# A fifth Strassen chunk per SwiGLU, with the products reordered and the next norms moved between them

## Chip, cores and metric

The kernel runs on one core of a Trainium2 chip. The metric is the device time of one execution in microseconds (us); before the change its median over 3 runs is 1292.14 us (1290.93 to 1292.8).

## The reference, cut to what matters

One decoder layer on 512 tokens of width 1024, all in float32. Two SwiGLU sub-layers stand around a token mixer:

```python
def swiglu(x, w_gate, w_up, w_down):
    return (jax.nn.silu(x @ w_gate) * (x @ w_up)) @ w_down

x = x + 0.5 * swiglu(rms_norm(x, ffn1_norm), ffn1_w_gate, ffn1_w_up, ffn1_w_down)
x = x + token_mixer(rms_norm(x, mix_norm), w_in, ...)
x = x + 0.5 * swiglu(rms_norm(x, ffn2_norm), ffn2_w_gate, ffn2_w_up, ffn2_w_down)
```

The hidden width of a SwiGLU (D_FF) is 2816, that is 22 blocks of 128.

## The kernel before

**Arithmetic.** Every float32 product of matrices is made of three matmuls (`mm3`, line 502): each operand is split into a high part (rounded to fp32r) and a low part (the rest), and high x high, high x low and low x high are added up in PSUM. So each weight tile is first split: ScalarE (ACT) writes the high part `whi` (line 106), and VectorE (DVE) or GpSimd (POOL) subtracts it from the raw tile to get the low part `wlo` (line 107). The order on each engine is that in which the Python code issues its instructions; nothing is moved by a scheduler.

**The SwiGLU (`ffn`, line 564).** Pass p = 0 to 10 of the loop at line 659 makes 256 hidden columns: two "gate" blocks g0, g1 and two "up" blocks u0, u1, of 24 matmuls each (128 x 128 by 128 x 512). `act_g` and `act_u` turn each pair into a hidden block `a` (line 583), which is split in turn into the left operands of the down projection. The 22 hidden blocks are multiplied with w_down in two ways:

- Blocks 0 to 15 in four **chunks** of four blocks each, by Strassen's seven products over a 2 x 2 cut of (tokens: tiles 0, 1 / tiles 2, 3) and (output columns: 0 to 511 / 512 to 1023). A product (`down_block`, line 633) is 2 groups of 6 matmuls and is added to one or two quarters of x (`INTO`, line 631; `add_x`, line 643). Chunk c is worked off in passes 2c + 2 and 2c + 3, one product behind each gate or up block (4 in the even pass, 3 in the odd). Its weights come through `Blocks` (line 127): two raw tiles of 1 MB each, seven parts, of which some are sums or differences of quarters that POOL computes ahead of the split (`sum`, line 149; `after`, line 152); the low parts of these weights are always made on POOL (line 93).
- Blocks 16 to 21 plainly (`down_tile`, line 646): blocks 16 and 17 (weights d4) within pass 10, 48 matmuls between g1 and u0; blocks 18 to 21 (weights d5_0, d5_1) in the closing loop at line 699, 24 matmuls for each of the four token tiles.

**The order of the splits.** `plan` lists all weight parts in the order in which PE uses them. `W.get` (line 115) issues every split up to the part asked for, if that has not been done; `W.bg(n)` (line 121) issues one more split, if no more than n parts beyond the current one have been issued. Within a SwiGLU each block and each product calls it once with n = 2, so that splits are issued two parts ahead of their use; in pass 10 it is called with n = 4, twice for each up block. `whi` and `wlo` have four buffers each; the parts in `W.held` (line 397) go to buffers of the large pool in their place. So a split can wait for the matmuls of the part that had its buffer, and what is queued behind it on ACT or DVE waits with it. In `down_block` the call of `W.bg` (line 636) stands ahead of the product's matmuls and additions.

**Between the first SwiGLU and the mixer.** When a token tile of x is whole, `after1` (line 742) queues three stages in `nstage`: `norm_1` (sum of squares on ACT, mean on DVE, a power on POOL), `norm_2` (two multiplications on DVE that write h) and `norm_3` (eight transposes `nt` on PE, split into hmh and hml by ACT and DVE). Each `tick` runs the next stage of every queued tile. The closing loop calls `tick` twice for each token tile, and `W.bg(4)` behind it. The mixer begins with `proj_c` (line 797), whose weights are the parts of c0 and c1. Behind the second SwiGLU `after2` only writes the tile out. PSUM has three banks for each of `mm` (line 265) and `sc` (line 268); `down_tile` and one half of `down_block` use `sc`, and a bank is free again when its additions on DVE are done.

Of the kernel before, what the change touches and what calls it, by code (L numbers as in the profile page):

```python
# [12 lines left out]
F32R = mybir.dt.float32r  # L13
AF = mybir.ActivationFunctionType
ALU = mybir.AluOpType
# [5 lines left out]
NT = SEQ // 128  # L21
# [105 lines left out]
class Blocks:  # L127
# [15 lines left out]
    def part(self, p):  # L143
        if p == 0:
            self.spare = self.new_spare()
            self.sum(self.spare, self.b12, self.b22, ALU.subtract)
        return (self.spare, self.b11, self.b22, self.spare, self.b12, self.b11, self.b21)[p]

    def sum(self, out, a, b, op):
        self.nc.gpsimd.tensor_tensor(out, a, b, op=op)  # L150
# [1 line left out]
    def after(self, p):  # L152
        if p == 1:
            self.sum(self.spare, self.b11, self.b22, ALU.add)
        elif p == 2:
            self.sum(self.b12, self.b11, self.b12, ALU.add)
        elif p == 3:
            self.sum(self.b11, self.b21, self.b11, ALU.subtract)
        elif p == 4:
            self.sum(self.b21, self.b21, self.b22, ALU.add)  # L160
        elif p == 6:
            self.then()

# [70 lines left out]
def drain(g):  # L234
    for _ in g:
        pass
# [8 lines left out]
def hybrid_trunk_kernel(ctx: ExitStack, tc: tile.TileContext, x, rel_bias, ffn1_norm, ffn1_w_gate, ffn1_w_up,  # L245
# [28 lines left out]
    def t4(name, dt=F32):  # L274
        return big.tile([128, 1024], dt, tag="t4", name=name)
# [12 lines left out]
    specs, plan, blocks = [], [], {}  # L288
# [20 lines left out]
    def rows(w, name, r0, nk, c0, nc_):  # L309

        src = w[r0:r0 + nk * 128, c0:c0 + nc_].rearrange("(k p) c -> p k c", p=128)
        loads = [(lambda raw: raw[:, :nk * nc_].rearrange("p (k c) -> p k c", k=nk), src)]
        parts = [lambda raw, h=h: raw[:, :nk * nc_].rearrange("p (k c) -> p k c", k=nk)
                 [:, h * nk // 2:(h + 1) * nk // 2, :] for h in range(2)]
        add_spec(loads, parts, name)

    def ffn_specs(f):
        wg, wu, wd = ffn_w[f]
        for c in range(4):
            src = wd[c * 512:c * 512 + 512].rearrange("(k p) c -> p k c", p=128)  # L320
            blocks[f"w{f}{c}"] = Blocks(
                nc, lambda h, c=c: big2.tile([128, 4, 512], F32, tag="hT", name=f"raww{f}{c}{h}"),
                lambda c=c: t4(f"rawe{f}{c}").rearrange("p (k c) -> p k c", k=2),
                [src[:, :, h * 512:h * 512 + 512] for h in range(2)],
                lambda c=c: c < 3 and blocks[f"w{f}{c + 1}"].load())
        for p in range(11):
            between = p in range(2, 10)
            cols(wg, f"g{f}{p}", 256 * p, not between)
            if p == 10:
                rows(wd, f"d{f}4", 16 * 128, 2, 0, 1024)  # L330
            cols(wu, f"u{f}{p}", 256 * p, not between)
            if between:
                for i, (kind, j) in enumerate((("g", 0), ("g", 1), ("u", 0), ("u", 1))):
                    plan.append((f"{kind}{f}{p}", j))
                    if p % 2 * 4 + i < 7:
                        plan.append((f"w{f}{p // 2 - 1}", p % 2 * 4 + i))
        for h in range(2):
            rows(wd, f"d{f}5_{h}", (18 + 2 * h) * 128, 2, 0, 1024)

    ffn_specs(0)  # L340
    def c_view(raw):
        return raw[:, :4 * C_W].rearrange("p (k c) -> p k c", k=4)

    for i in range(2):
        src = w_in[512 * i:512 * i + 512]
        add_spec([(lambda raw, o=o, n=n: c_view(raw)[:, :, o:o + n],
                   src[:, c:c + n].rearrange("(k p) c -> p k c", p=128))
                  for o, c, n in ((0, C_Q, 384), (384, IDX_K, 72))],
                 [lambda raw, h=h: c_view(raw)[:, 2 * h:2 * h + 2, :] for h in range(2)], f"c{i}")
    for j in range(2):  # L350
        cols256(w_in, f"iq{j}", IDX_Q + 256 * j)

# [41 lines left out]
        rows(w_out, f"wo{n}", 256 * n, 2, 0, 1024)  # L394
    ffn_specs(1)
    W = Weights(nc, rawp, wsp, specs, plan, blocks, 2)
    W.held, W.held_tile = [(n, p) for n in ("d05_0", "d15_0", "wo2", "c0") for p in range(2)], lambda name: t4(name, F32R)


    xt = [t4(f"x{t}") for t in range(NT)]  # L400
# [149 lines left out]
    ALL = slice(0, SEQ)  # L550
# [13 lines left out]
    def ffn(f, hT, order, hooks, after_tile):  # L564

        aT = {}

        def mm_in(kind, p, j, ps, s):
            wh, wl = W.get(f"{kind}{f}{p}", j)
            for k, _ in enumerate(mm3(ps[:, s], [(wh[:, k, :], wl[:, k, :]) + hk(hT, k, s) for k in range(KD)])):  # L570
                if p == 10 and kind == "u" and k % 12 == 0 or p and k == 0:
                    W.bg(4 if p == 10 else 2)

        def act_g(ff, g):
            th = tmp.tile([128, 512], F32, tag="z", name=f"th{f}{ff}")
# [5 lines left out]
        def act_u(ff, m, u):  # L581
            a = tmp.tile([128, 512], F32, tag="p", name=f"a{f}{ff}", bufs=6)
            nc.vector.tensor_tensor(a, m, u, op=ALU.mult)  # L583
            if ff < 16:
                left_blocks(ff, a)
                return
            if ff % 2 == 0:
                aT[ff // 2, "pair"] = (t4k(f"ah{f}{ff}"), t4k(f"al{f}{ff}"))
            pair = aT[ff // 2, "pair"]
            aT[ff] = (pair[0][:, ff % 2, :], pair[1][:, ff % 2, :])  # L590
            split(aT[ff][0], aT[ff][1], a)
# [30 lines left out]
        def left(c, pr, i, u):  # L622
            cs = slice(128 * u, 128 * u + 128)
            if i == 0:
                return tuple(aT["a11", c][:, pr, x, cs] for x in range(2))
            if i in (2, 5):
                cs = slice(cs.start + 256, cs.stop + 256) if i == 5 else cs
                return tuple(aT["a_2", c, pr][:, x, cs] for x in range(2))
            return tuple(hl[:, {1: 0, 3: 1, 4: 3, 6: 2}[i], cs] for hl in aT["s", c, pr])

        INTO = ((0, 1, 1), (1, 1, 1)), ((1, 0, 1), (1, 1, -1)), ((0, 0, -1), (0, 1, 1)), ((0, 0, 1), (1, 1, 1)),             ((1, 1, 1),), ((0, 0, 1), (1, 0, 1)), ((0, 0, 1),)

        def down_block(c, i):

# [11 lines left out]
        def down_tile(t, k0, parts, hook=None):  # L646
            for half in range(2):
                ps = sc(f"dn{f}{k0}{half}{t}")
                csl = slice(512 * half, 512 * half + 512)
                terms = []  # L650
                for k, w in enumerate(parts):
                    ah, al = aT[k0 + k]
                    terms.append((ah[:, tok(t)], al[:, tok(t)], w[0][:, 0, csl], w[1][:, 0, csl]))
                drain(mm3(ps, terms))
                if half == 0 and hook is not None:
                    hook()
                add_x(ps, t, csl)

        for p in range(11):
            ps, ms = {}, {}  # L660
            step = 0
            if p == 1:
                blocks[f"w{f}0"].load()
            W.cap = W.first[f"u{f}0", 1] if p == 0 else 1 << 30
            todo = order if p == 0 else [("g", 0, ALL), ("g", 1, ALL), None, ("u", 0, ALL), ("u", 1, ALL)]
            for item in todo:
                if item is None:
                    if p == 10:
                        parts = [W.get(f"d{f}4", k) for k in range(2)]
                        for t in range(NT):  # L670
                            if t % 2 == 0:
                                W.bg()
                            down_tile(t, 16, parts)
                    continue
                if callable(item):
                    item()
                    continue
                kind, j, s = item
                if (kind, j) not in ps:
                    ps[kind, j] = (mm if kind == "g" else sc)(f"{kind}{f}{p}{j}")  # L680
                mm_in(kind, p, j, ps[kind, j], s)
                while late:
                    late.pop()()
                if p == 0 and s.stop == SEQ:
                    W.cap += 1
                    W.split(W.cap)
                if s.stop == SEQ:
                    if kind == "g":
                        ms[j] = act_g(2 * p + j, ps["g", j])
                    else:  # L690
                        act_u(2 * p + j, ms[j], ps["u", j])
                if p in range(2, 10):
                    if p % 2 * 4 + step < 7:
                        down_block(p // 2 - 1, p % 2 * 4 + step)
                    step += 1
            if p in hooks:
                hooks[p]()
        parts = [W.get(f"d{f}5_{k // 2}", k % 2) for k in range(4)]
        for t in range(NT):
            down_tile(t, 18, parts, nstage.tick)  # L700
            after_tile(t)
            nstage.tick()
            W.bg(4)


    nstage = Stages()
# [759 lines left out]
```

## Time and profile before

| what | value |
|---|---|
| runs | 1290.93, 1292.14, 1292.8 us |
| profiled execution: its time / its span | 1292.1 / 1290.0 us |
| granted TensorE clock, mean | 0.994 |
| PE (matmul) busy | 1273.0 us, 99% of the span, 6880 matmuls |
| DVE busy | 798.7 us, 62% |
| ACT busy | 484.1 us, 38% |
| POOL busy | 475.8 us, 37% |

The span is the time from the first to the last recorded instruction of one execution; 2.1 us of its time lie around it. A matmul's recorded duration covers its way through the pipeline, so the cost of one matmul more is read from the distance of the starts of a row of them, not from the duration of one. The lines that bear on the change are shown in the section on rows below.

### The profile page before, as it was taken

How to read it: one execution, taken by the hardware profiler on the slowest of the kernel's cores; microseconds unless marked ns; L12 is line 12 of the kernel's file. 1: busy time of each engine (PE TensorE's matmuls, PEld its weight loads, DVE VectorE, ACT ScalarE, POOL GpSimd, SP SyncE). 2: the span in 40 equal slices, each digit the busy share in tenths (PEclk: the TensorE clock that was granted, in tenths of full speed). 3: DMA queues.
4: the chain of work that ended last, by engine and by line, in shares of the span. 5: the costliest groups of instructions: out<-in, count | busy, mean ns of one | idle time of the engine just before them, and what ended most of it. 6: DMA issues, size and time to landing. Idle time of an engine off the chain costs nothing. (4 is left out here: it accounts for less than half of the span.)

```text
span 1290.0 us, 17385 instructions
## 1 busy us (share of the span) xinstructions
PE 1273.0 (99%) x6880; PEld 1081.7 (84%) x6880; DVE 798.7 (62%) x1377; ACT 484.1 (38%) x872; POOL 475.8 (37%) x313
## 2 busy tenths in 40 slices
PE   9999999999999999999999999999999999999998
PEld 8888888888889889889887778888898888888887
DVE  4467777765573766597854554446645767676553
ACT  4242333332243555454556432224233333333220
POOL 2475757561011444446440000000015756666500
PEclk9999999999999999999989999999999999999999
DMA  5424141422433222222221034433332233333131
GB/s 196 141 69 139 57 162 37 161 69 82 137 126 96 60 81 79 87 66 83 66 83 46 33 103 147 131 96 101 98 108 89 98 99 102 112 108 103 66 98 66
DMA packets 101779, 125.08 MB, mean 97 GB/s; under 512 B 3817, under 2 KB 85225, under 8 KB 101698
## 3 DMA queue, kind: packets, MB, share of 16 engines
q1 hardware_dynamic: 96690, 114.08, 27.2%
q10 hardware_dynamic: 3456, 5.24, 1.3%
q0 software_dynamic: 1552, 4.65, 1.1%
q8 instruction: 54, 0.88, 0.3%
q14 instruction: 27, 0.22, 0.1%
HBM read 119.13 MB, written 4.84 MB: 96 GB/s over the span
## 5 line engine op out<-in xcount | busy, mean ns | idle before, releaser
L107 DVE TENSOR_TENSOR wlo<-raw,whi 128x1024 fp32r<-128x1024 f32 (+1 forms) x146 | 219.7, 1510 | 61.3 <-ACT whi L106 61.0
L106 ACT ACTIVATE whi<-raw 128x1024 fp32r<-128x1024 f32 (+1 forms) x178 | 185.5, 1050 | 64.8 <-PE u L507 26.5
L644 DVE SCALAR_TENSOR_TENSOR x<-dn,x 128x512 f32<-128x512 f32 x224 | 143.4, 682 | 30.0 <-PE dn L507 27.5
L107 POOL TENSOR_TENSOR wlo<-raww,whi 128x1024 fp32r<-128x1024 f32 x40 | 99.5, 2487 | 96.6 <-ACT whi L106 96.6
L583 DVE TENSOR_TENSOR a<-m,u 128x512 f32<-128x512 f32 x44 | 30.2, 687 | 101.8 <-PE u L507 101.8
L107 POOL TENSOR_TENSOR wlo<-raw,whi 128x1024 fp32r<-128x1024 f32 x32 | 76.7, 2395 | 29.0 <-ACT whi L106 25.1
L576 ACT ACTIVATE th<-g 128x512 f32<-128x512 f32 x44 | 26.2, 595 | 143.2 <-PE g L507 143.1
L507 PE MATMUL gt<-rmh,wlo 128*128 128x512 f32 x192 | 76.2, 397 | 0.0
L507 PE MATMUL gt<-rml,whi 128*128 128x512 f32 x192 | 76.0, 396 | 0.0
L507 PE MATMUL gt<-rmh,whi 128*128 128x512 f32 x192 | 76.0, 396 | 0.0
L507 PE MATMUL g<-hah,whi 128*128 128x512 f32 (+1 forms) x192 | 71.6, 373 | 0.2 <-ACT hah L512 0.2
L507 PE MATMUL g<-hal,whi 128*128 128x512 f32 (+1 forms) x192 | 71.4, 372 | 0.3 <-DVE hal L513 0.3
L507 PE MATMUL g<-hah,wlo 128*128 128x512 f32 (+1 forms) x192 | 71.4, 372 | 0.1
L507 PE MATMUL u<-hbh,wlo 128*128 128x512 f32 (+1 forms) x192 | 71.4, 372 | 0.0
L507 PE MATMUL u<-hah,wlo 128*128 128x512 f32 (+1 forms) x192 | 71.4, 372 | 0.0
L507 PE MATMUL g<-hbh,whi 128*128 128x512 f32 (+1 forms) x192 | 71.4, 372 | 0.0
L507 PE MATMUL u<-hah,whi 128*128 128x512 f32 (+1 forms) x192 | 71.4, 372 | 0.0
L507 PE MATMUL u<-hbh,whi 128*128 128x512 f32 (+1 forms) x192 | 71.4, 372 | 0.0
L507 PE MATMUL g<-hbl,whi 128*128 128x512 f32 (+1 forms) x192 | 71.3, 372 | 0.0
L507 PE MATMUL g<-hbh,wlo 128*128 128x512 f32 (+1 forms) x192 | 71.3, 371 | 0.0
L507 PE MATMUL u<-hbl,whi 128*128 128x512 f32 (+1 forms) x192 | 71.3, 371 | 0.0
L507 PE MATMUL u<-hal,whi 128*128 128x512 f32 (+1 forms) x192 | 71.3, 371 | 0.0
(1111 smaller groups left out, 3493.3 us busy)
## 6 DMA issues: line engine op xcount, KB each, us to landing
raw<-in_w_in SPq DMA_DIRECT2D x25, 1024.0 KB, 5.1
raw<-in_ffn_w_gate SPq DMA_DIRECT2D x22, 1024.0 KB, 5.1
raw<-in_ffn_w_up SPq DMA_DIRECT2D x22, 1024.0 KB, 5.2
raww<-in_ffn_w_down SPq DMA_DIRECT2D x16, 1024.0 KB, 6.1
raw<-in_ffn_w_down SPq DMA_DIRECT2D x6, 1024.0 KB, 5.0
raw<-in_w_in SPq DMA_DIRECT2D x8, 512.0 KB, 4.5
raw<-in_w_out SPq DMA_DIRECT2D x4, 1024.0 KB, 4.9
x<-in_x SPq DMA_DIRECT2D x4, 512.0 KB, 6.2
```

The costliest lines, as they stand in the source:

```text
L106: nc.scalar.activation(h, src, AF.Copy)
L107: sub.tensor_tensor(l, src, h.bitcast(F32), op=ALU.subtract)
L507: nc.tensor.matmul(ps, l, r, start=i == 0 and q == 0, stop=i == n - 1 and q == 2)
L576: nc.scalar.activation(th, g, AF.Tanh, scale=0.5)
L583: nc.vector.tensor_tensor(a, m, u, op=ALU.mult)
L644: nc.vector.scalar_tensor_tensor(xt[t][:, csl], ps, 0.25 * sign, xt[t][:, csl], op0=ALU.mult, op1=ALU.add)
```

## The change

- Blocks 16 to 19 become a fifth chunk (c = 4). Its products 0 to 3 run in pass 10, behind g0, g1, u0 and u1; d4 falls away there. The plain part is left with blocks 20 and 21 (weights d5, 2 parts).
- The seven products stand in another order, so that products 0 to 4 hold all that goes to the upper half of the tokens (tiles 0 and 1); products 5 and 6 go to tiles 2 and 3 alone. The sums that POOL makes of the weights follow that order.
- The closing loop becomes: product 4; plain tile 0; plain tile 1; product 5; product 6; plain tiles 2 and 3. A plain tile has 12 matmuls in place of 24. `nstage.tick` is called once behind each plain tile and once between products 5 and 6, where it was called twice for each tile.
- In pass 10 `W.bg` is called with n = 3: once for a gate block, twice for an up block. The plan ends, in the first SwiGLU, with u1, product 3, c0 (first part), product 4, c0 (second part), d5 (two parts), product 5, product 6, c1; in the second it is the same without c0 and c1. The parts of d5 are no longer among the held ones.

```diff
@@ class Blocks
-        return (self.spare, self.b11, self.b22, self.spare, self.b12, self.b11, self.b21)[p]
+        return (self.spare, self.b22, self.spare, self.spare, self.b21, self.b11, self.b12)[p]
...
         if p == 1:
             self.sum(self.spare, self.b11, self.b22, ALU.add)
         elif p == 2:
+            self.sum(self.spare, self.b21, self.b11, ALU.subtract)
+        elif p == 3:
+            self.sum(self.b21, self.b21, self.b22, ALU.add)
+        elif p == 4:
             self.sum(self.b12, self.b11, self.b12, ALU.add)
-        elif p == 3:
-            self.sum(self.b11, self.b21, self.b11, ALU.subtract)
-        elif p == 4:
-            self.sum(self.b21, self.b21, self.b22, ALU.add)
@@ the plan
+    def products(p, i):
+
+        return range(p % 2 * 4 + i, min(p % 2 * 4 + i + 1, 7))
...
-        for c in range(4):
+        for c in range(5):
...
-            between = p in range(2, 10)
+            between = p > 1
             cols(wg, f"g{f}{p}", 256 * p, not between)
-            if p == 10:
-                rows(wd, f"d{f}4", 16 * 128, 2, 0, 1024)
             cols(wu, f"u{f}{p}", 256 * p, not between)
             if between:
                 for i, (kind, j) in enumerate((("g", 0), ("g", 1), ("u", 0), ("u", 1))):
                     plan.append((f"{kind}{f}{p}", j))
-                    if p % 2 * 4 + i < 7:
-                        plan.append((f"w{f}{p // 2 - 1}", p % 2 * 4 + i))
-        for h in range(2):
-            rows(wd, f"d{f}5_{h}", (18 + 2 * h) * 128, 2, 0, 1024)
+                    plan.extend((f"w{f}{p // 2 - 1}", q) for q in products(p, i))
+        plan.extend([("c0", 0), (f"w{f}4", 4), ("c0", 1)] if f == 0 else [(f"w{f}4", 4)])
+        rows(wd, f"d{f}5", 20 * 128, 2, 0, 1024)
+        plan.extend((f"w{f}4", q) for q in (5, 6))
...
-    W.held, W.held_tile = [(n, p) for n in ("d05_0", "d15_0", "wo2", "c0") for p in range(2)], lambda name: t4(name, F32R)
+    W.held, W.held_tile = [(n, p) for n in ("wo2", "c0") for p in range(2)], lambda name: t4(name, F32R)
@@ ffn
-                if p == 10 and kind == "u" and k % 12 == 0 or p and k == 0:
-                    W.bg(4 if p == 10 else 2)
+                if p and k == 0 or p == 10 and kind == "u" and k == 12:
+                    W.bg(3 if p == 10 else 2)
...
-            if ff < 16:
+            if ff < 20:
                 left_blocks(ff, a)
                 return
...
-        INTO = ((0, 1, 1), (1, 1, 1)), ((1, 0, 1), (1, 1, -1)), ((0, 0, -1), (0, 1, 1)), ((0, 0, 1), (1, 1, 1)),             ((1, 1, 1),), ((0, 0, 1), (1, 0, 1)), ((0, 0, 1),)
+        INTO = (((0, 1, 1), (1, 1, 1)), ((0, 0, -1), (0, 1, 1)), ((0, 0, 1), (1, 1, 1)), ((0, 0, 1), (1, 0, 1)),
+                ((0, 0, 1),), ((1, 0, 1), (1, 1, -1)), ((1, 1, 1),))
...
-            todo = order if p == 0 else [("g", 0, ALL), ("g", 1, ALL), None, ("u", 0, ALL), ("u", 1, ALL)]
+            todo = order if p == 0 else [("g", 0, ALL), ("g", 1, ALL), ("u", 0, ALL), ("u", 1, ALL)]
...
-                if p in range(2, 10):
-                    if p % 2 * 4 + step < 7:
-                        down_block(p // 2 - 1, p % 2 * 4 + step)
+                if p > 1:
+                    for q in products(p, step):
+                        down_block(p // 2 - 1, q)
                     step += 1
...
-        parts = [W.get(f"d{f}5_{k // 2}", k % 2) for k in range(4)]
-        for t in range(NT):
-            down_tile(t, 18, parts, nstage.tick)
+
+        down_block(4, 4)
+        parts = [W.get(f"d{f}5", k) for k in range(2)]
+        for t, q in ((0, None), (1, 5), (2, None), (3, None)):
+            down_tile(t, 20, parts)
             after_tile(t)
             nstage.tick()
             W.bg(4)
+            if q:
+                down_block(4, q)
+                nstage.tick()
+                down_block(4, q + 1)
```

## Rows read from the trace of the kernel before

**Rows 1.** The page, busy time of each engine (share of the span, instructions).

```profile
PE 1273.0 (99%) x6880; PEld 1081.7 (84%) x6880; DVE 798.7 (62%) x1377; ACT 484.1 (38%) x872; POOL 475.8 (37%) x313
```

**Rows 2.** The chain that ended last, second SwiGLU's end: start, us, what.

```profile
1242.57 10.88 PE dn L507 x48
...
1264.33 21.83 PE dn L507 x96
...
1286.17 0.69 DVE x L644
```

**Rows 3.** Waits of PE: longest one (us in total, times, longest).

```profile
PE a2kt L781 <- ACT a2qk L782: 2.1, 1, 2.1
```

**Rows 4.** Engine table, first closing loop: length, PE, PEld, DVE, ACT, POOL busy; clock.

```profile
345.00:368.30 23.30, 23.30 (x113) 19.39 (x112) 15.70 (x25) 8.59 (x14) 1.66 (x3) 1.00 0.45 153
```

**Rows 5.** Timeline of SP, load of chunk 3's two raw tiles.

```profile
226.54 11.30 SPq L139 DMA_DIRECT2D raww<-in_ffn_w_down  x2
```

**Rows 6.** Timeline of DVE in pass 8 of the first SwiGLU.

```profile
259.42 3.23 DVE L107 TENSOR_TENSOR wlo<-raw,whi 128x1024 fp32r<-128x1024 f32 x1
...
267.27 1.22 DVE L107 TENSOR_TENSOR wlo<-raw,whi 128x1024 fp32r<-128x1024 f32 x1
271.50 0.69 DVE L583 TENSOR_TENSOR a<-m,u 128x512 f32<-128x512 f32 x1 [3.02 <-PE u L507]
272.89 0.69 DVE L513 TENSOR_TENSOR al<-a,ah 128x512 fp32r<-128x512 f32 x1 [0.70 <-ACT ah L512]
273.50 2.48 DVE L644 SCALAR_TENSOR_TENSOR x<-dn,x 128x512 f32<-128x512 f32 x4
275.89 1.49 DVE L107 TENSOR_TENSOR wlo<-raw,whi 128x1024 fp32r<-128x1024 f32 x1
```

**Rows 7.** Timeline of POOL in the same pass.

```profile
259.16 2.40 POOL L150 TENSOR_TENSOR rawe<-raww,raww 128x1024 f32<-128x1024 f32 x1
264.97 2.41 POOL L107 TENSOR_TENSOR wlo<-raww,whi 128x1024 fp32r<-128x1024 f32 x1 [3.40 <-ACT whi L106]
267.32 3.41 POOL L150 TENSOR_TENSOR raww<-raww,raww 128x1024 f32<-128x1024 f32 x1
273.88 2.41 POOL L107 TENSOR_TENSOR wlo<-rawe,whi 128x1024 fp32r<-128x1024 f32 x1 [3.15 <-ACT whi L106]
```

**Rows 8.** Timeline of ACT in the same pass.

```profile
263.84 1.05 ACT L106 ACTIVATE whi<-raww 128x1024 fp32r<-128x1024 f32 x1
...
272.23 0.63 ACT L512 ACTIVATE ah<-a 128x512 fp32r<-128x512 f32 x1 [6.39 <-DVE a L583]
```

**Rows 9.** Timeline of DVE, closing loop of the first SwiGLU, token tile 0.

```profile
350.38 0.69 DVE L644 SCALAR_TENSOR_TENSOR x<-dn,x 128x512 f32<-128x512 f32 x1 [2.03 <-PE dn L507]
...
353.15 1.11 DVE L107 TENSOR_TENSOR wlo<-raw,whi 128x912 fp32r<-128x912 f32 x1 [0.70 <-ACT whi L106]
354.17 1.41 DVE L534 SCALAR_TENSOR_TENSOR h<-x,nr10r,gain 128x512 f32<-128x512 f32 x2
...
356.90 1.29 DVE L513 TENSOR_TENSOR hml<-nt,hmh 128x512 fp32r<-128x512 f32 x2
```

**Rows 10.** Timeline of ACT, same loop and tile.

```profile
351.11 1.06 ACT L528 ACTIVATE sq<-x 128x1024 f32<-128x1024 f32 x1 [4.81 <-DVE x L644]
...
352.17 0.95 ACT L106 ACTIVATE whi<-raw 128x912 fp32r<-128x912 f32 x1
```

**Rows 11.** The chain that ended last, transposes of one norm.

```profile
922.12 0.87 PE nt L543 x8
```

**Rows 12.** Engine table around that wait: length, PE busy; granted clock third from the end.

```profile
661.00:662.00 1.00, 0.00 (x0) 0.00 (x0) 0.00 (x0) 0.63 (x2) 0.00 (x0) 1.00 0.72 131
...
663.00:664.00 1.00, 1.00 (x9) 1.00 (x9) 0.28 (x1) 0.69 (x2) 0.81 (x1) 0.81 0.07 21
664.00:665.00 1.00, 0.92 (x5) 0.62 (x3) 1.00 (x3) 0.00 (x0) 1.00 (x1) 0.50 0.00 0
...
670.00:671.00 1.00, 1.00 (x9) 1.00 (x8) 1.00 (x5) 0.02 (x1) 1.00 (x1) 0.78 0.00 0
```

More of the change, by code (lines that the diff above doesn't have):

```diff
@@ L324, in ffn_specs @@
                 [src[:, :, h * 512:h * 512 + 512] for h in range(2)],
-                lambda c=c: c < 3 and blocks[f"w{f}{c + 1}"].load())
+                lambda c=c: c < 4 and blocks[f"w{f}{c + 1}"].load())
         for p in range(11):
-            between = p in range(2, 10)
+            between = p > 1
             cols(wg, f"g{f}{p}", 256 * p, not between)
-            if p == 10:
-                rows(wd, f"d{f}4", 16 * 128, 2, 0, 1024)
             cols(wu, f"u{f}{p}", 256 * p, not between)
@@ L348, in hybrid_trunk_kernel @@
                   for o, c, n in ((0, C_Q, 384), (384, IDX_K, 72))],
-                 [lambda raw, h=h: c_view(raw)[:, 2 * h:2 * h + 2, :] for h in range(2)], f"c{i}")
+                 [lambda raw, h=h: c_view(raw)[:, 2 * h:2 * h + 2, :] for h in range(2)], f"c{i}", i > 0)
     for j in range(2):
@@ L625, in left @@
                 return tuple(aT["a11", c][:, pr, x, cs] for x in range(2))
-            if i in (2, 5):
-                cs = slice(cs.start + 256, cs.stop + 256) if i == 5 else cs
+            if i in (1, 3):
+                cs = slice(cs.start + 256, cs.stop + 256) if i == 3 else cs
                 return tuple(aT["a_2", c, pr][:, x, cs] for x in range(2))
-            return tuple(hl[:, {1: 0, 3: 1, 4: 3, 6: 2}[i], cs] for hl in aT["s", c, pr])
-        INTO = ((0, 1, 1), (1, 1, 1)), ((1, 0, 1), (1, 1, -1)), ((0, 0, -1), (0, 1, 1)), ((0, 0, 1), (1, 1, 1)),             ((1, 1, 1),), ((0, 0, 1), (1, 0, 1)), ((0, 0, 1),)
+            return tuple(hl[:, {5: 0, 2: 1, 6: 3, 4: 2}[i], cs] for hl in aT["s", c, pr])
+        INTO = (((0, 1, 1), (1, 1, 1)), ((0, 0, -1), (0, 1, 1)), ((0, 0, 1), (1, 1, 1)), ((0, 0, 1), (1, 0, 1)),
+                ((0, 0, 1),), ((1, 0, 1), (1, 1, -1)), ((1, 1, 1),))
         def down_block(c, i):
@@ L664, in ffn @@
             W.cap = W.first[f"u{f}0", 1] if p == 0 else 1 << 30
-            todo = order if p == 0 else [("g", 0, ALL), ("g", 1, ALL), None, ("u", 0, ALL), ("u", 1, ALL)]
+            todo = order if p == 0 else [("g", 0, ALL), ("g", 1, ALL), ("u", 0, ALL), ("u", 1, ALL)]
             for item in todo:
-                if item is None:
-                    if p == 10:
-                        parts = [W.get(f"d{f}4", k) for k in range(2)]
-                        for t in range(NT):
[L671 to L674, printed above, removed]
                 if callable(item):
@@ L697, in ffn @@
                 hooks[p]()
-        parts = [W.get(f"d{f}5_{k // 2}", k % 2) for k in range(4)]
-        for t in range(NT):
-            down_tile(t, 18, parts, nstage.tick)
+        down_block(4, 4)
+        parts = [W.get(f"d{f}5", k) for k in range(2)]
+        for t, q in ((0, None), (1, 5), (2, None), (3, None)):
+            down_tile(t, 20, parts)
             after_tile(t)
```

## Prediction, written before the changed kernel was run

> **What bounds the kernel now.** I read the busy times first, then the chain that ended last, then the waits of PE, then the closing loop of a SwiGLU engine by engine. Matmuls fill 99% of the span [rows 1], and the chain through the second SwiGLU's end is PE alone: 48 matmuls of the plain part in 10.88 us, 96 in 21.83 us [rows 2]. One matmul thus costs 10.88/48 = 0.227 us, six of one group 1.36, twelve 2.72, a gate or up block of 24 5.44 us. PE's longest wait anywhere is 2.1 us, in the mixer [rows 3]. In the first SwiGLU's closing loop PE is busy for 23.30 of 23.30 us at the full clock, DVE for 15.70, ACT for 8.59, POOL for 1.66 [rows 4]. The reader is to see two things: matmuls taken out are worth their full time, if PE goes on finding its operands; and the closing loop hides a chain of norms behind tiles of 24 matmuls, which the change halves.
>
> **Removed matmuls.** Four hidden blocks cost 96 plain matmuls or 7 x 12 = 84 in a chunk. Two SwiGLUs save 24: 24 x 0.227 = **-5.4 us**. The count is certain.
>
> **Work added beside PE up to pass 10.** Per SwiGLU DVE makes 24 + 8 additions in place of 16, some 0.62 us each (2.48 for four) [rows 6]; 9 weight parts are split where 6 were, ACT 1.05 us each [rows 8]; 7 low parts and 5 sums, about 2.4 us each, come onto POOL [rows 7]. The two 1 MB raw tiles replace two 1 MB loads on SP's queue, at the place where chunk 3's stand, which keep it for 11.30 us [rows 5]. All this stands in passes 8 to 10 as chunk 3 and its forerunners do in their passes, where the list of PE's waits has no line, so I cost it at 0. Without that cover one late part would cost up to its split, 1.05 + 2.4 us. The new product order needs a sum directly behind the part before it: one was ready at 259.16 + 2.40 = 261.56, its split began at 263.84 [rows 7, 8]. 0 again.
>
> **The rule of the lock.** A subtraction on DVE took 3.23 us from 259.42, while POOL's sum ran from 259.16 to 261.56; undisturbed it takes 1.22. It ended 1.1 us behind POOL's. Another, at 267.27, came first, and POOL's sum took 3.41 in place of 2.41. Four additions from PSUM beside POOL's subtraction at 273.88 took their 2.48 us all the same [rows 6, 7]. So DVE's operations between two SBUF tiles and POOL's exclude each other; those that read PSUM go on. Now POOL works within the closing stretch, where it had nothing but powers.
>
> I follow each engine's order from U, the end of u1 in pass 10; pass 8 gives the positions (its u0 ends at 271.48, 8.16 before its U). PE then wants product 3 until 2.72, product 4 until 5.44, tile 0 until 8.16, and so on.
>
> **First SwiGLU, wait A: the split of d5.** By the calls of `W.bg`, u1 issues c0 (first) and part 4, product 4 issues c0 (second), and d5 only comes with `W.get` behind product 4. DVE works in that order. POOL: low part of part 3 until -5.3, sum until -2.5 (held up by DVE's `al`), then ACT's split of part 4, its low part until 1.0, the next sum until 3.4. DVE: `a` at 0.0, its split on ACT until 1.4, `al` held by that sum until 3.9; four additions of product 3 until 6.3; c0's low part (1.11 [rows 9]) until 7.4; two additions of product 4 until 8.6; d5's low parts at 9.75 and 10.9. PE takes one matmul (high x high) at 5.44 and then waits from 5.67 to 9.75 and again 0.45: **+4.5 us**. Without the lock the parts come at 7.9 and 9.1: +2.8.
>
> **Wait B: product 5.** Its split is issued behind tile 0's norm. Tile 0 ends at 12.7; addition 0.69, square 1.06 [rows 9, 10], high part 1.05, low part on POOL 2.4 [rows 7, 8]: 17.9. Tile 1 ends at 15.4, and product 5's second matmul is due at 15.65: **+2.25 us**. The order square, then split is that of before [rows 10].
>
> **Waits C and D: DVE's backlog.** Ahead of product 5's additions DVE has c1's low part, and c1's high part needs a buffer that product 5 itself holds: 20.4 + 1.0 + 1.1 = 22.5. Behind it queue four additions, `hml` 1.29 and the next h 1.41 [rows 9]: h is there at 27.7. PE has done transposes (0.87 [rows 11]), product 6 and tile 2 by 26.7: +1.0. After those transposes tile 3 needs the `sc` bank of product 6, whose additions stand behind c1's second part: 30.05 for 28.6, +1.45. Together **+2.45**. What is late next is tile 3's norm, covered by two C tiles. First SwiGLU: +9.2.
>
> One thing rows don't show is the multiplication h (both inputs in SBUF) beside POOL; I take 0. The Trainium skill (SBUF — State Buffer, "Who interferes with whom") has any DVE instruction with two SBUF inputs contend with a GpSimd instruction that reads SBUF. No run here shows that for h. By it h, the power and product 6's low part come later, and my estimate of the whole would be 0.6 us more.
>
> **Second SwiGLU.** No norms, no c0. d5's first part is issued within u1, but DVE's subtraction is held by POOL's low part of part 4 until 2.15 and stands ahead of `a`; `al` waits for the next sum until 4.95, the additions of product 3 end at 7.4, and d5's second low part waits for POOL's low part of part 5 until 7.85: ready at 8.95, due at 6.35: **+2.65** (+0.1 without the lock). Then splits are ahead, and additions keep pace.
>
> **The clock.** Behind the 2.1 us wait of rows 3 the granted clock fell from 1.00 to 0.50 (2.4 to 1.2 GHz) at about 663.6 and was back at about 670.4 [rows 12], some 6.9 us. A matmul at the low level takes twice its time, so 3.4 us are lost where PE is never idle. Waits of 4.1 and 2.65 us are longer than that one. Bounds per SwiGLU 0 and 3.4; I take 2.2 in the first, where part of it replaces wait B, and 2.3 in the second (two thirds): **+4.5**.
>
> **Sum.** -5.4 + 9.2 + 2.65 + 4.5 = +10.95. From the profiled execution's 1292.1 us, which is the median of the runs: **1303.0 us**. Without lock and clock: first SwiGLU 2.8 + 2.25 + 2 = 7.1, second 0.1: +1.8, 1293.9. With the clock's full price in both and once more in the first: 6.4 + 3.4 + 3.4 + 3.4 = +16.6, 1308.7. The likeliest case's own range is 1298 to 1309.
>
> **Rivals.** (1) *Faster, 1286.7 us* (-5.4): the low parts of d5 reach PE before product 4 ends. It decides at one point: DVE must have d5's first part done within 0.23 us of that end. For it: DVE is busy for 62% only [rows 1], and in the loop of before nothing was late [rows 4]. Against: in the issue order product 4's last addition (0.69), which can't begin before PE ends, stands ahead of the 1.22 us subtraction, so 1.7 us of wait remain in the first SwiGLU even for an idle DVE. (2) *Late but cheap, 1294 to 1298*: waits as listed, but `al` slips in between POOL's two operations (margin 0.4 us), and no fall of the clock. (3) *A draw*: the first SwiGLU loses what the second saves, 1290 to 1294; for that B, C and D would have to be absent, the norms being ready as the new order means them to be. That fewer matmuls are issued isn't in doubt.
>
> **How the numbers follow.** Forecast 0.60, rival 2 0.18, faster 0.14, draw 0.06, beyond 1309 0.02. A difference of 0.2% (2.6 us) is about what a measurement of this kernel can tell from none. Slower by more: the forecast, beyond and all but the low edge of rival 2, 0.79; within 0.07; faster 0.14. The range leaves out faster, half of the draw and what is above: 1293 to 1309.
>
> **What would show it.** In the changed trace: PE's waits name DVE `wlo` under `dn` behind product 4 (4 us first, 2 to 3 us second SwiGLU) and POOL `wlo` under product 5 (about 2 us); `al` behind u1 takes over 2 us; `nt` waits for h by 1 us; the clock's row shows 0.5 near both ends; matmuls number 24 fewer; passes 8 and 9 show no PE wait. I'm wrong if PE stays busy through either closing stretch, or if the clock holds at 1.00 through the waits.

## The result, and the profile after

The changed kernel takes 1301.68 us (median of 6 runs, 1301.16 to 1303.09), the kernel before 1291.54 in 6 runs beside it: 1.0082 times as long, 95% interval 1.0071 to 1.0093, so 9.2 to 12.0 us slower. The profiled execution took 1303.09 us with a span of 1301.3, 11.3 longer than that of before; its mean granted clock is 0.991. It is the slowest of the six, so some of what is read from it below isn't in the difference of the medians, 1301.68 - 1291.54 = 10.1 us. One execution behind the numbers of the experiments took 2519.83 us: it is one of the ten of experiment 1, and the only one of them with a trace.

The page, busy time of each engine (before: [rows 1]):

```profile
PE 1274.4 (98%) x6856; PEld 1079.8 (83%) x6856; DVE 838.7 (64%) x1405; ACT 494.9 (38%) x882; POOL 554.2 (43%) x357
```

The 24 matmuls are gone. The waits of PE over the whole span (us in total, times, longest), where before the longest of all was [rows 3]:

```profile
PE dn L509 <- DVE wlo L107: 6.7, 2, 4.1
...
PE dn L509 <- POOL wlo L107: 1.9, 1, 1.9
...
PE dn L509 <- DVE x L647: 1.5, 1, 1.5
...
PE nt L545 <- DVE h L536: 0.2, 1, 0.2
```

A wait in this view counts from the modelled end of the matmul before it. What the path loses is read from starts. The timeline of PE (start, duration, what) in the first SwiGLU's closing stretch and in the second's:

```profile
347.30 0.39 PE L509 MATMUL dn<-whi,ah 128*128 128x512 f32 x1
351.81 0.50 PE L509 MATMUL dn<-wlo,ah 128*128 128x512 f32 x1 [4.13 <-DVE wlo L107]
...
358.61 0.39 PE L509 MATMUL dn<-whi,al 128*128 128x512 f32 x1
359.20 0.50 PE L509 MATMUL dn<-whi,sh 128*128 128x512 f32 x1 [0.20 <-ACT whi L106]
361.64 0.50 PE L509 MATMUL dn<-wlo,sh 128*128 128x512 f32 x1 [1.94 <-POOL wlo L107]
...
372.00 0.39 PE L509 MATMUL dn<-whi,al 128*128 128x512 f32 x1
372.61 1.29 PE L545 MATMUL nt<-ident,h 128*128 128x128 f32 x8 [0.22 <-DVE h L536]
375.40 0.50 PE L509 MATMUL dn<-whi,ah 128*128 128x512 f32 x1 [1.50 <-DVE x L647]
...
383.25 1.04 PE L545 MATMUL nt<-ident,h 128*128 128x128 f32 x8
...
1277.15 0.39 PE L509 MATMUL dn<-whi,ah 128*128 128x512 f32 x1
1280.09 0.50 PE L509 MATMUL dn<-wlo,ah 128*128 128x512 f32 x1 [2.55 <-DVE wlo L107]
```

From each distance the undisturbed one is taken off, 0.23 us for a matmul and 0.87 for the transposes [rows 11]. Wait A, d5 behind product 4: 351.81 - 347.30 - 0.23 = 4.3. Wait B, product 5: 361.64 - 358.61 - 0.45 = 2.6. C, the transposes: 372.61 - 372.00 - 0.23 = 0.4 ahead of the first four, and 1.29 - 1.04 = 0.25 ahead of the last four, which need the second h (it ends at 371.72 + 1.40 = 373.12): 0.6. D, tile 3: 375.40 - 372.61 - 0.87 - 0.25 = 1.7. Second SwiGLU: 1280.09 - 1277.15 - 0.23 = 2.7.

The clock, from the engine table in slices of 1 us (length, PE, PEld, DVE, ACT and POOL busy; the granted clock stands third from the end; 1.00 is 2.4 GHz, 0.50 is 1.2):

```profile
352.00:353.00 1.00, 1.00 (x4) 0.44 (x3) 0.90 (x1) 0.00 (x0) 0.00 (x0) 0.60 1.06 398
353.00:354.00 1.00, 1.00 (x4) 0.81 (x4) 0.00 (x0) 0.00 (x0) 0.00 (x0) 0.50 0.80 193
354.00:355.00 1.00, 1.00 (x4) 0.81 (x3) 0.69 (x1) 0.00 (x0) 0.00 (x0) 0.50 0.79 162
355.00:356.00 1.00, 1.00 (x5) 0.78 (x4) 0.00 (x0) 0.00 (x0) 0.00 (x0) 0.69 1.07 378
...
362.00:363.00 1.00, 1.00 (x5) 0.81 (x4) 0.86 (x3) 0.00 (x0) 0.06 (x1) 0.72 0.00 0
363.00:364.00 1.00, 1.00 (x4) 0.81 (x3) 0.00 (x0) 0.00 (x0) 1.00 (x2) 0.50 0.00 0
364.00:365.00 1.00, 1.00 (x4) 0.71 (x4) 0.00 (x0) 0.00 (x0) 1.00 (x1) 0.50 0.00 0
365.00:366.00 1.00, 1.00 (x5) 0.70 (x4) 0.00 (x0) 0.00 (x0) 0.83 (x1) 0.57 0.00 0
...
1280.00:1281.00 1.00, 0.91 (x3) 0.80 (x4) 1.00 (x3) 0.00 (x0) 1.00 (x1) 0.81 0.00 0
1281.00:1282.00 1.00, 1.00 (x4) 0.71 (x4) 0.84 (x2) 0.00 (x0) 1.00 (x1) 0.50 0.06 16
1282.00:1283.00 1.00, 1.00 (x4) 0.81 (x3) 0.00 (x0) 0.00 (x0) 0.28 (x1) 0.50 0.28 109
1283.00:1284.00 1.00, 1.00 (x4) 0.81 (x3) 0.52 (x1) 0.00 (x0) 0.00 (x0) 0.50 0.40 154
```

In each of the three stretches, behind A, behind B and behind the second SwiGLU's wait, PE has no gap once it has its operands, so what is missing to 1.00 in a slice is counted as lost (in the rows above a matmul starts every 0.23 us at 1.00, and in the same timeline every 0.43 at 0.50): 0.40 + 0.50 + 0.50 + 0.31 = 1.7 us, and 1.7 in the two others, together 5.1.

The sum: -5.4 (matmuls) + 9.2 (A to D) + 2.7 + 5.1 = +11.6; the spans differ by 11.3. The stretches of low clock that lie in the mixer are the same in both traces (two of 3.4 us and one of 6.8), so they all but drop out of the difference. The first matmul of `iq` in the mixer starts 9.9 us later than before (400.7 for 390.8), that of `wo` 9.6 (898.9 for 889.3): between the two ends the distance hardly changes.

Now the engines that make PE wait. The timeline of DVE in the first closing stretch:

```profile
343.45 2.57 DVE L515 TENSOR_TENSOR al<-a,ah 128x512 fp32r<-128x512 f32 x1 [0.70 <-ACT ah L514]
345.94 2.47 DVE L647 SCALAR_TENSOR_TENSOR x<-dn,x 128x512 f32<-128x512 f32 x4
348.34 1.09 DVE L107 TENSOR_TENSOR wlo<-raw,whi 128x912 fp32r<-128x912 f32 x1
349.35 1.28 DVE L647 SCALAR_TENSOR_TENSOR x<-dn,x 128x512 f32<-128x512 f32 x2
350.55 2.34 DVE L107 TENSOR_TENSOR wlo<-raw,whi 128x1024 fp32r<-128x1024 f32 x2
...
359.65 3.15 DVE L536 SCALAR_TENSOR_TENSOR h<-x,nr10r,gain 128x512 f32<-128x512 f32 x2
...
367.10 1.11 DVE L107 TENSOR_TENSOR wlo<-raw,whi 128x912 fp32r<-128x912 f32 x1 [4.24 <-ACT whi L106]
...
371.72 1.40 DVE L536 SCALAR_TENSOR_TENSOR h<-x,nr11r,gain 128x512 f32<-128x512 f32 x2
```

And of POOL:

```profile
343.06 2.41 POOL L150 TENSOR_TENSOR raww<-raww,raww 128x1024 f32<-128x1024 f32 x1
...
359.22 2.37 POOL L107 TENSOR_TENSOR wlo<-raww,whi 128x1024 fp32r<-128x1024 f32 x1 [0.20 <-ACT whi L106]
```

The reader is to see the queue behind wait A: `al` (0.69 us in [rows 6]) takes 2.57 and ends 0.5 us behind POOL's sum (343.06 + 2.41 = 345.47); behind it stand four additions, c0's low part, two additions, and only then d5's low parts, which PE has wanted since 347.5.

At the second SwiGLU's end DVE is held in the same way: a subtraction of a weight part takes 1.22 us undisturbed and `al` 0.69 [rows 6], and here

```profile
1270.81 2.53 DVE L107 TENSOR_TENSOR wlo<-raw,whi 128x1024 fp32r<-128x1024 f32 x1 [2.01 <-issue]
...
1274.64 1.51 DVE L515 TENSOR_TENSOR al<-a,ah 128x512 fp32r<-128x512 f32 x1 [0.70 <-ACT ah L514]
...
1278.47 1.57 DVE L107 TENSOR_TENSOR wlo<-raw,whi 128x1024 fp32r<-128x1024 f32 x1
```

The last of the three makes the part that PE waits for: it ends at 1280.04, and PE goes on at 1280.09.

### The profile page after: what moved, and what is told of

It is laid out like the page before. It is cut to its first block, busy times and chain, and to the rows that moved or that the text cites. A ratio compares the mean times of both kernels' runs of the same rounds, so it can differ in the third digit from the quotient of the medians.

```text
span 1301.3 us, 17477 instructions
## 1 busy us (share of the span) xinstructions
PE 1274.4 (98%) x6856; PEld 1079.8 (83%) x6856; DVE 838.7 (64%) x1405; ACT 494.9 (38%) x882; POOL 554.2 (43%) x357
## 3 DMA queue, kind: packets, MB, share of 16 engines
HBM read 119.13 MB, written 4.84 MB: 95 GB/s over the span
## 5 line engine op out<-in xcount | busy, mean ns | idle before, releaser
L106 ACT ACTIVATE whi<-raw 128x1024 fp32r<-128x1024 f32 (+1 forms) x170 | 177.6, 1049 | 47.3 <-PE g L509 16.7
L647 DVE SCALAR_TENSOR_TENSOR x<-dn,x 128x512 f32<-128x512 f32 x256 | 162.8, 682 | 18.3 <-PE dn L509 15.5
L107 POOL TENSOR_TENSOR wlo<-rawe,whi 128x1024 fp32r<-128x1024 f32 x30 | 72.1, 2405 | 50.8 <-ACT whi L106 50.8
L509 PE MATMUL dn<-whi,a 128*128 128x512 f32 x240 | 78.8, 389 | 0.0
L602 POOL TENSOR_TENSOR sum<-a 128x256 f32<-128x256 f32 x40 | 29.6, 739 | 111.4 <-DVE a L585 89.9
```

The costliest lines, as they stand in the source:

```text
L106: nc.scalar.activation(h, src, AF.Copy)
L107: sub.tensor_tensor(l, src, h.bitcast(F32), op=ALU.subtract)
L509: nc.tensor.matmul(ps, l, r, start=i == 0 and q == 0, stop=i == n - 1 and q == 2)
L602: plus = lambda out, l, r, op=ALU.add: nc.gpsimd.tensor_tensor(out, l, r, op=op)
L647: nc.vector.scalar_tensor_tensor(xt[t][:, csl], ps, 0.25 * sign, xt[t][:, csl], op0=ALU.mult, op1=ALU.add)
```

## Experiments

Times are medians; "+x" is the difference from the kernel before, run on the same chip in the same session. By that the change itself stands at 1301.68 - 1291.54 = +10.1.

**1. The new product order without the fifth chunk.** Four chunks in both SwiGLUs, with the old closing loop, plan and pass 10:

```diff
-        for c in range(5):
+        for c in range(5 if FIVE[f] else 4):
...
-            if ff < 20:
+            if ff < (20 if FIVE[f] else 16):
```

with FIVE = (False, False).

> Four chunks in both SwiGLUs, as before, with the new order of the seven products and of the sums of weights. My theory (all of the loss lies in the two closing stretches): no difference from before, 1291.5 us within 1 us, no PE wait named dn. Rival (the new product order itself costs, because a sum stands directly ahead of the part that needs it): slower than before by some us, with PE waits in passes 2 to 9.

1290.46 beside 1291.22, ratio 0.9993 (0.9984 to 1.0003). The order and POOL's sums behind one another cost nothing that can be measured, as the prediction's 0 for the product order has it. This rests on the times; PE's waits can't be read for this run.

**2 and 3. The fifth chunk in the second SwiGLU alone, and in the first alone.** The same edit with FIVE = (False, True) and (True, False).

> The fifth chunk in the second SwiGLU alone. My theory: 12 matmuls less (-2.7 us), a wait of 2.6 us behind product 4 and some 1.6 us at the lower clock: 1293 us, 1 to 2.5 us above before. Rival (a closing stretch without norms hides everything): -2.7 us, 1288.8.

> The fifth chunk in the first SwiGLU alone. My theory: waits of about 8 us and two falls of the clock of 1.7 us each against 2.7 us saved: 8.5 to 10 us above before, 1300 to 1301.5; with the run of the second SwiGLU alone it adds up to the whole change. Rival (the two ends are coupled, or the loss is spread over the passes): the two don't add up to 10 us.

The second alone: 1291.52, ratio 1.0001 (0.9991 to 1.001), +0.3; PE's list has `dn` behind DVE `wlo` with 2.5 us, and the clock reads 0.50 from 1269 to 1272. The first alone: 1300.33, ratio 1.0068 (1.0053 to 1.0083), +9.1, with the same 4.1, 1.9 and 1.5 us of waits as the whole change. 0.3 + 9.1 = 9.4 for the whole's 10.1: the two ends add up, within what the medians can tell. The second SwiGLU's gain is eaten at its own end; the first does the damage. The second alone cost less than the 1 to 2.5 us expected, and less than its steps in the change, -2.7 + 2.7 + 1.7 = +1.7, which lies outside its interval (-1.2 to +1.3); why is open. In the trace of the first alone the clock fell at 350.4, within wait A, and was back at 357.0: 6.8 us in place of 3.4, of which PE worked 4.8, so 2.4 us lost in place of 1.7.

**4. Block 21's `al` on POOL**, where it queues behind the sum in place of being held by it:

```diff
-            split(aT[ff][0], aT[ff][1], a)
+            nc.scalar.activation(aT[ff][0], a, AF.Copy)
+            (nc.gpsimd if ff == 21 else nc.vector).tensor_tensor(aT[ff][1], a, aT[ff][0].bitcast(F32), op=ALU.subtract)
```

> The changed kernel, with the low part of the last hidden block (128x512) subtracted on POOL in place of DVE. My theory (DVE's subtraction is held by POOL's sum, and with it all of DVE's queue): first wait 4.1 to about 2.6 us, second wait 2.6 to under 1 us with no fall of the clock behind it: 4 to 5 us faster than the changed kernel, 1296.5 to 1298. Rival (no lock; DVE just has 0.7 us too much work there): at most 0.7 us in each SwiGLU, 1300.3.

1294.25, ratio 1.0029 (1.0018 to 1.004), +3.0: 7.1 us come back, more than expected. The waits of PE and its timeline at that place:

```profile
PE dn L509 <- DVE wlo L107: 3.0, 3, 2.4
```

```profile
350.18 0.50 PE L509 MATMUL dn<-wlo,ah 128*128 128x512 f32 x1 [2.37 <-DVE wlo L107]
...
1272.69 0.50 PE L509 MATMUL dn<-wlo,ah 128*128 128x512 f32 x1 [0.45 <-DVE wlo L107]
```

Wait A falls from 4.13 to 2.37 (+0.17 for the second part, a wait that the list of the change does not have, since PE is slow there), that of the second SwiGLU from 2.55 to 0.45: 3.7 us of waiting. The other 3.4 are the clock: in this execution it is 1.00 behind A and at the second end, and falls once only, behind B (0.50 from 360 to 363). So one 0.69 us subtraction and its hold, taken out of DVE's queue, were worth some 7 us, about half of it through the clock. The subtraction's own time is at most 0.7 us of wait in each SwiGLU (the rival), so most of the 3.7 is the hold; no run moves the hold alone. Behind this 2.4 us wait the clock seems to fall in some executions only: four of the seven runs took 1293.6 to 1294.3 at a mean clock of 0.997, three 1296.3 to 1297.3 at 0.993 to 0.995. Only the first kind was profiled.

**5. PE kept busy through the waits.** 16 matmuls without use behind product 4 in the first SwiGLU and 10 in the second, and 8 ahead of product 5 in the first, into a PSUM bank that nothing reads:

```diff
+        def busy(n, name):
+            ps = tr(name)
+            for _ in range(n):
+                nc.tensor.matmul(ps, aT[20][0][:, tok(0)], hT[0][0][:, 0, :], start=True, stop=True)
         down_block(4, 4)
+        busy((10, 16)[f == 0], f"busya{f}")
...
```

> The changed kernel with matmuls that nobody reads laid into the waits: 16 behind product 4 and 8 ahead of product 5 in the first SwiGLU, 10 behind product 4 in the second. My theory (each wait is followed by about 3.4 us at 1.2 GHz, which costs 1.7 us): the clock stays at 1.00 in both stretches, 4 to 5 us faster than the changed kernel, about 1297. Rival (the slow matmuls only fill time in which PE would have waited anyway): the clock stays up and the time is that of the changed kernel, 1301.7, or more.

1298.62, ratio 1.006 (1.0045 to 1.0075), +7.8: 2.3 us less than the change, between theory and rival; the two profiled spans differ by 4.6 (1301.3 - 1296.7), of which up to 1.7 is a fall of the clock in the mixer (at 543 us) that only the change's trace has. The clock is 1.00 throughout both stretches. Timeline of PE:

```profile
347.39 3.79 PE L697 MATMUL busya<-hah,ah 128*128 128x512 f32 x16
...
351.89 0.50 PE L509 MATMUL dn<-wlo,ah 128*128 128x512 f32 x1 [0.48 <-DVE wlo L107]
353.02 0.50 PE L509 MATMUL dn<-wlo,ah 128*128 128x512 f32 x1 [0.16 <-DVE wlo L107]
...
364.78 0.50 PE L509 MATMUL dn<-wlo,sh 128*128 128x512 f32 x1 [0.35 <-POOL wlo L107]
...
372.87 0.50 PE L509 MATMUL dn<-whi,ah 128*128 128x512 f32 x1 [1.50 <-DVE x L647]
```

The d5 part is no earlier (351.89 for 351.81), so what is saved is the clock's. Tile 3 begins 2.5 us earlier (372.87 for 375.40), not 3.4: waits come up at 353.02 and 364.78 that a slow PE never reached. Time at the low clock is thus partly time that PE would have waited anyway.

**6. d5 ahead of product 4's additions:**

```diff
-        down_block(4, 4)
         parts = [W.get(f"d{f}5", k) for k in range(2)]
+        down_block(4, 4)
```

> The changed kernel with the splits of d5 asked for ahead of product 4; part 5's split is then issued within product 4, ahead of the norms. My theory (order and lock together): in the first SwiGLU the wait for product 5 goes (-1.9) with its fall of the clock (-1.7), but POOL now subtracts part 5 where DVE wants to subtract c0 and d5, so the first wait does not shrink (4.1 to 4.6 us): about 1298. Rival (order alone): the first wait shrinks by product 4's two additions, 1.3 us, and the second goes: 1296 to 1296.5.

1297.96, ratio 1.0053 (1.0038 to 1.0068), +7.2, as expected. Wait A stays at 4.0; the second end keeps its 2.5 us; wait B and the clock's fall behind it are gone, because the call within product 4 now already issues product 5's split. DVE's timeline shows why A stays:

```profile
343.61 2.56 DVE L515 TENSOR_TENSOR al<-a,ah 128x512 fp32r<-128x512 f32 x1 [0.70 <-ACT ah L514]
...
348.49 4.45 DVE L107 TENSOR_TENSOR wlo<-raw,whi 128x912 fp32r<-128x912 f32 x3
```

The two additions are out of d5's way, but POOL's low part of product 5 (347.35, 2.36 us) now runs beside the three subtractions and holds them: 4.45 us for 1.1 + 2 x 1.22 = 3.5. Taking one item out of a late queue gave its place to another hold.

**7. c1's split out of products 5 and 6:**

```diff
-            W.bg()
+            if c < 4 or i < 5:
+                W.bg()
```

> The changed kernel without the call that issues one more split within products 5 and 6; the two parts of c1 are then issued behind plain tiles 2 and 3. My theory (their wait for product 5's buffers holds ACT and DVE, and DVE's backlog keeps tile 3's PSUM bank): the wait of 1.5 us named DVE x goes, 1 to 2 us faster than the changed kernel, about 1300. Rival (that wait only shows DVE's load as such): no difference.

1300.82, ratio 1.0076 (1.0061 to 1.0092), +10.0, not to be told from the change, where 1 to 2 us less were expected. The waits of PE say where D went:

```profile
PE c L509 <- DVE wlo L107: 0.7, 1, 0.7
PE c L509 <- ACT whi L106: 0.6, 1, 0.6
```

The 1.5 us wait for `x` is gone, which shows that c1's split in DVE's queue made it; the split is then late for `proj_c`. It has to go somewhere else, not merely later.

**8. The closing stretch in another order.** `al` of block 21 on POOL as in 4; d5's first part planned ahead of product 4; c0 behind the down projection's parts; product 5's and 6's splits issued right behind d5; the split at the end of each turn of the loop gone, so that c0 is split by the calls within products 5 and 6 and both parts of c1 behind tile 2; the low parts of c0 and c1 on POOL:

```diff
-        plan.extend([("c0", 0), (f"w{f}4", 4), ("c0", 1)] if f == 0 else [(f"w{f}4", 4)])
         rows(wd, f"d{f}5", 20 * 128, 2, 0, 1024)
+        plan.insert(-1, (f"w{f}4", 4))
...
         parts = [W.get(f"d{f}5", k) for k in range(2)]
+        W.bg(4)
+        W.sub = nc.gpsimd if f == 0 else nc.vector
         for t, q in ((0, None), (1, 5), (2, None), (3, None)):
             down_tile(t, 20, parts)
+            if t == 2:
+                W.bg(4)
+                W.bg(4)
             after_tile(t)
             nstage.tick()
-            W.bg(4)
...
```

(with one more split in product 3, `W.bg(3)`).

> The fifth chunk in both SwiGLUs with the queues put in another order: d5's first part is split ahead of part 4's and the second within product 3; parts 5 and 6 ahead of the norms; c0 and c1 within products 5 and 6 and behind tile 2, their low parts on POOL; the last hidden block's low part on POOL. My theory (all that was lost is order): under 2 us of waits are left at the two ends, no fall of the clock, 1287 to 1289. Rival (DVE and POOL together have too much work in these stretches): waits of 4 us or more remain, 1291 or above.

1287.17 beside 1290.79, ratio 0.9974 (0.9963 to 0.9985), -3.6: faster than both kernels. Waits A, B and the second SwiGLU's are gone, and the clock is 1.00 in both stretches. Two timelines, DVE's and POOL's, show what is left:

```profile
359.11 4.84 DVE L536 SCALAR_TENSOR_TENSOR h<-x,nr11r,gain 128x512 f32<-128x512 f32 x2
```

```profile
356.35 9.63 POOL L107 TENSOR_TENSOR wlo<-raw,whi 128x912 fp32r<-128x912 f32 x4
```

The two multiplications h, 1.41 us in [rows 9], take 4.84 beside POOL's low parts, and the transposes wait 1.2 us for them; the list has 0.8 us more, for additions (0.6 in the first stretch, 0.2 in the second). -5.4 + 2.0 = -3.4 for the -3.6 measured.

**9. That order in the second SwiGLU alone.**

> The fifth chunk and the reordered queues in the second SwiGLU alone, the first as before. My theory (each end gives its own 2.7 us, less what waits are left): no wait above 0.3 us at the second end, 2.4 to 2.7 us below before, about 1288.3; the reordered first end then has given the rest of the 3.6 us that both gave together. Rival (the whole gain of both comes from the second end): 1287.2.

1288.06 beside 1290.78, ratio 0.9979 (0.997 to 0.9989), -2.7. The 12 matmuls that one SwiGLU saves are worth 12 x 0.227 = 2.7 us: with nothing late (PE's list has 0.2 us at that end), the saving is paid out in full, within an interval of 1.4 to 3.9 us. The edit is that of 8, with FIVE = (False, True) as in 2.

**10. As 8, with the low parts of c0 and c1 on DVE:**

```diff
-        W.sub = nc.gpsimd if f == 0 else nc.vector
+        W.sub = nc.vector
```

> The reordered kernel with the low parts of c0 and c1 on DVE again. My theory (POOL's four subtractions hold the multiplication h of tile 1, but DVE's queue is fuller without POOL): the wait of 1.2 us for h shrinks to under 0.5 us, while additions run later and tile 3's bank or c1's low parts are waited for, 1 to 2 us; in sum the same time within 1 us, 1287 to 1288. Rival (POOL's lock is the dearer of the two): 1 us or more faster, 1286.

1286.47 beside 1290.78, ratio 0.9965 (0.9952 to 0.9978), -4.3, the lowest median of all; its gain over 8 lies within the intervals, so theory and rival are not told apart by the time. The waits of PE and the engine table of the stretch:

```profile
PE dn L509 <- DVE x L648: 1.4, 2, 1.2
```

```profile
360.00:370.00 10.00, 8.78 (x44) 7.36 (x43) 10.00 (x16) 3.02 (x5) 0.55 (x1) 1.00 0.55 174
```

h is no longer held, and no transposes wait for it. DVE is now busy for all of these 10 us, and what PE still waits for (1.2 us before tile 3) is an addition at the end of that queue, a wait of the same kind as D. -5.4 + 1.4 = -4.0 for the -4.3 measured.

## Why the prediction was right

By its own steps, predicted against read from the starts:

| step | predicted, us | measured, us |
|---|---|---|
| 24 matmuls less | -5.4 | -5.4 |
| wait A, split of d5 | +4.5 | +4.3 |
| wait B, product 5 | +2.25 | +2.6 |
| C, transposes behind h | +1.0 | +0.6 |
| D, tile 3's bank | +1.45 | +1.7 |
| second SwiGLU | +2.65 | +2.7 |
| clock | +4.5 | +5.1 |
| sum | +10.95 | +11.6 |

The measured sum is that of the traced execution, 11.3 us by the spans; by the medians the change costs 10.1.

- **A and the lock.** The order on DVE is the predicted one, item by item, and `al` ends when POOL's sum lets it. Experiment 4 tests it: with `al` off DVE, A is 2.9 us by starts (2.53 and 0.34 for the second part), where the step had 2.8 without the lock. The 0.45 us that the step had for the second part did not show in the change, since PE was at the low clock there. Rival 2, `al` slipping in between POOL's operations, did not happen.
- **B** stands where it was put, behind tile 0's square and POOL's low part. Experiment 6 removes it by issuing the split one call earlier.
- **C and D.** D has the predicted cause: DVE stands 4.24 us idle for c1's split on ACT and does its additions behind it; experiment 7 takes the wait away with that split. Their division is a little off: C 0.4 us shorter than worked out, D 0.2 longer, together 2.3 for 2.45. With the clock held, in experiment 5, PE's list has no wait of transposes for h, and PE waits for product 6's low part in their place; why h fell behind less was not tried by itself.
- **The rule for h was taken the wrong way.** The prediction took 0 where the Trainium skill (SBUF — State Buffer, "Who interferes with whom") has a DVE instruction with two SBUF inputs contend with a GpSimd instruction that reads SBUF. The trace agrees with the skill: h took 3.15 us beside POOL's low part, for 1.41 alone, and 4.84 in experiment 8. In the changed kernel it cost nothing, since the transposes of that tile stood behind the slow product 5; in experiment 8 it was the wait that was left.
- **The clock** was sized as one partial fall in each SwiGLU, between 0 and 3.4 us. It was two in the first and one in the second, each 1.7 us, so the sum of the term came out by luck and its parts did not: the falls are shorter than the one of [rows 12], and wait B, 1.9 us in the list, had one too. The 3.4 us was also a bound and not the cost of that fall, in which PE stood idle for about 1 us (665 to 666).
- **The second SwiGLU** has the predicted holds one by one. The prediction's own figures give 8.95 - 6.35 = 2.60 there, not 2.65.
- **Passes 8 and 9** show no PE wait, and experiment 1 finds the product order free. The row given for that 0 doesn't support it, though: the split at 263.84 in [rows 8] reads `raww`, not the `rawe` that the sum at 259.16 wrote [rows 7], whose split came at 272.76. In the changed kernel a split does wait for the sum directly ahead of it, and PE still has what it needs:

```profile
339.56 1.07 ACT L106 ACTIVATE whi<-raww 128x1024 fp32r<-128x1024 f32 x1 [2.71 <-POOL raww L150]
```

- **The draw and the faster case.** That the second SwiGLU would save its 2.7 us (the draw) fell: alone it gains nothing. That an idle DVE would still leave 1.7 us of A standing in this issue order was not tried; experiment 4, which takes `al` off DVE, leaves 2.4 us, and A went only when experiments 8 and 10 changed the order too.

How often the clock falls behind a wait of about 2 us can be counted in the mixer, where the eleven traces of the two kernels and of experiments 2 to 10 have the wait of [rows 3], 1.9 to 2.5 us long: in seven of them the clock then stood at 0.50 for 3.4 us, in three for 6.8, and in one (experiment 6, 2.0 us) it did not fall. What decides between these was not tried.

## What to carry to other kernels

Where PE is busy to the last per cent, fewer matmuls are worth their full time only if the operands come as early as before: write down, for the stretch that gets shorter, the in-order queue of each helper engine from a known point, with the holds between DVE and POOL in it, and compare it with the matmuls' due times. That list forecast every wait of the changed kernel to within half a microsecond, and reordering it turned 10 us of loss into 4 us of gain. Waits of the size seen here (1.9 to 4.1 us on a busy PE) should be priced with the clock behind them: 1.7 us each in the changed kernel, 2.4 us or nothing for the same place in other runs, and a part of it may be time that would have been waited for anyway.

## What was not expected of the hardware

- The multiplication h, a three-operand instruction of DVE with two tiles in SBUF, is held by POOL just as plain subtractions are: 3.15 and 4.84 us for 1.41.
- The granted clock fell to 0.50 behind a wait that the list gives as 1.9 us (B) and behind one of 2.5, and stayed at 1.00 in the profiled execution of experiment 4 behind one of 2.4. The length of the wait alone doesn't decide it.
- The low stretches at the two ends of the changed kernel lasted 3.4 us each, half as long as the one of [rows 12] in the mixer, and cost 1.7 us each; the one behind wait A in experiment 3 lasted 6.8.
